# Gate and up products of a gated MLP as seven block products instead of eight, with features and residual kept in DRAM

## The chip, the cores and the metric

The kernel runs on one core of one Trainium2 chip. The metric is device time in microseconds, from the first to the last instruction and what little lies around it; lower is better. One profiled execution supplies the trace.

A core has TensorE (PE, the matrix engine, which writes to the eight banks of PSUM), VectorE (DVE), ScalarE (ACT), GpSimd (POOL) and SyncE (SP), which here issues the DMAs. Each engine runs its own instructions in their order and waits on semaphores. "PEld" are TensorE's weight loads, which lie beside its matmuls.

## The reference

One decoder layer for 1024 tokens of 1024 channels, in float32: a token mixer (two recurrent branches), a layer norm, a gated MLP with a short causal convolution, and a second layer norm. The change concerns the MLP and its surroundings:

```python
def conv_ffn(h, w_gate, w_up, conv_w, conv_b, w_down):
    gate = causal_dwconv(h @ w_gate, conv_w) + conv_b
    return (jax.nn.gelu(gate) * (h @ w_up)) @ w_down
...
x = layer_norm(DEEPNORM_ALPHA * x + (1.0 + gt1) * mix, ln1_g[l], ln1_b[l])
h = x * (1.0 + sc2) + sh2
ff = conv_ffn(h, ffn_w_gate[l], ffn_w_up[l], ffn_conv_w[l], ffn_conv_b[l], ffn_w_down[l])
x = layer_norm(DEEPNORM_ALPHA * x + (1.0 + gt2) * ff, ln2_g[l], ln2_b[l])
```

`D_FF` is 2816, so there are 22 feature tiles of 128; the convolution has three taps.

## The kernel before

Activations lie transposed: 128 channels on the partitions, tokens along the free dimension. There are KT = 8 channel tiles, and the 1024 tokens are cut into two halves of 512, which is what one PSUM bank holds.

**Three matmuls for one.** A float32 product is made of three passes in the type fp32r. `split` (L201, L202) makes from a tile `src` a rounded part `hi` on ACT and the rest `lo = src - hi` on DVE. `mm3` (L268 to L270) then issues hi x hi, hi x lo and lo x hi into one bank. `half_split` does the same for a tile of 512. Weights come by `load_w` (L262): a DMA to a raw buffer, of which there are three, then a split into one of two pairs of buffers, with a priority 1500 instructions ahead.

**Order.** The order of the instructions of each engine is not written out by hand here: a planner orders them when the program is built, by the order of the program (shifted by `high_priority(offset=...)`), by what is ready and by which buffers are free. The chip then keeps that order on each engine. A tile named by `half(...)` is one of 80 buffers of 512 floats in the pool of the third phase, which serves the merge of the two branches, the output projection, both layer norms and the MLP.

**The part before the MLP.** `ys[d][hf]` holds the residual of channel tile d and half hf. For each half, the output projection adds into `ys` (L1070), POOL adds up over d (L996), and `layer_norm_steps` is a generator that issues the norm in 18 steps: the mean by a matmul with a constant matrix (L1007, L1008), the subtraction (L1019), the squares (L1022) and for the second half their sum by 16 matmul instructions with the constant matrix (L1024), the inverse root (L1031, L1032), then for each d the multiplication by it (L1036 on DVE), scale and offset (L1044 on ACT) and `modulate` (L1057 on DVE, then `half_split`), which gives the MLP's input `h2_hi[d][hf]`, `h2_lo[d][hf]`. Callers place these steps between their own work by `steps(ln, n)`; the norm of half 1 lies beside the first feature tiles of half 0.

**The MLP.** The 22 feature tiles are worked in groups of 7, 7 and 8 (`FGROUPS`). `hidden(f, hf, w, carry)` does one tile and one half: the gate product (8 k tiles x 3 matmuls), its copy out of PSUM (L1092), three taps (L1097, L1100, where `carry` brings the last two columns of half 0 to half 1), the GELU on ACT (L1102), the up product, the product of both (L1106) and the split of the result. In the first group all seven tiles of half 0 come before those of half 1; in the second, both halves of a tile follow one another. `down` then multiplies a group's seven or eight feature tiles by a tile of `w_down` and adds into `ys` (L1124), one output tile d after another. The last group's half 0 is followed by its down projection and its norm, which lies beside the last group's half 1; half 1's down projection and norm come last, in two pieces of 256 tokens (`down_and_norm`).

Of the kernel before, what the change touches and what calls it, by code (L numbers as in the profile page):

```python
# [9 lines left out]
F32 = mybir.dt.float32  # L10
# [6 lines left out]
P = 128  # L17
# [14 lines left out]
FGROUPS = (7, 7, 8)  # L32
# [17 lines left out]
N_SIDE0 = 3  # L50
LN_EPS = 1e-5
# [40 lines left out]
def hybrid_layer_kernel(ctx: ExitStack, tc: tile.TileContext, xT, c, w_adaT, cols_in, rows_in,  # L92
# [819 lines left out]
    third = phase("third", 0, 80)  # L912
# [141 lines left out]

    def modulate(d, y, hf, lo):
        t = half("h2")
        V.tensor_scalar(out=t, in0=y, scalar1=mods[:, 16 + d : 17 + d], scalar2=adab[:, 24 + d : 25 + d],  # L1057
                        op0=ALU.mult, op1=ALU.add)
        h2_hi[d][hf], h2_lo[d][hf] = half_split(t)

    ln = iter(())
# [14 lines left out]

    groups = [list(range(sum(FGROUPS[:n]), sum(FGROUPS[: n + 1]))) for n in range(len(FGROUPS))]

    def conv_half():
        return cur["pool"].tile([P, HALF + 4], F32, tag="cv", bufs=4, name=nm("cv"))  # L1080

    def hidden(f, hf, w, carry):

        cv = conv_half()
        if carry is None:
            V.memset(cv[:, 0:4], 0.0)
        else:
            V.tensor_copy(out=cv[:, 2:4], in_=carry)
# [3 lines left out]
        A.activation(cv[:, 4 : 4 + HALF], ps, AF.Copy)  # L1092
        if hf + 1 < NHALF:
            carry = sm([P, 2], tag="carry", bufs=max(FGROUPS) + 1, name="carry")
            V.tensor_copy(out=carry, in_=cv[:, 2 + HALF : 4 + HALF])
        t = half("gate")
        V.tensor_scalar(out=t, in0=cv[:, 2 : 2 + HALF], scalar1=col("ffn_w", 3 * f), scalar2=col("ffn_b", f),  # L1097
                        op0=ALU.mult, op1=ALU.add)
        for i in range(1, 3):
            V.scalar_tensor_tensor(out=t, in0=cv[:, 2 + i : 2 + i + HALF], scalar=col("ffn_w", 3 * f + i), in1=t,  # L1100
                                   op0=ALU.mult, op1=ALU.add)
        A.activation(t, t, AF.Gelu_apprx_tanh)  # L1102
# [4 lines left out]
        return half_split(t), carry  # L1107

    def gate_up(f):
        return [load_w(w_gu[f, s], KT) for s in range(2)]  # L1110
# [4 lines left out]
    def down(fs, acts, d, parts, w=None):  # L1115

        w = w or load_down(fs, d)
# [39 lines left out]
    prev = None  # L1157
    for gi, fs in enumerate(groups):
        acts = [[None] * NHALF for _ in fs]
        ends = gi in (0, len(groups) - 1)  # L1160
        carries = [None] * len(fs)
# [99 lines left out]
```

## Time and the profile before

| | |
|---|---|
| time, median of 3 runs | 2551.51 us (2548.04 to 2556.07) |
| the profiled execution | 2552.6 us, its span 2550.9 us |
| mean granted TensorE clock in it | 0.982 |
| TensorE's matmuls | 11591 |
| output projection ends, MLP begins | about 1790 us into the span |
| last matmul of the down projection | about 2532 us into the span |

The page of the profile gives each engine's busy time and share of the span, then the same in 40 slices, the chain of work that ended last, and the costliest groups of instructions: line, engine, operation, output and inputs, count, then busy time, mean in ns, and the idle time of the engine just before them with what ended it. Busy time of TensorE is modelled (matmuls overlap), so the number of matmuls that start in a stretch says more than its busy share.

### The profile page before, as it was taken

Reading aid. Unit: us, or ns where it says so; the run is one execution under the profiler, and the core shown is the slowest. Engines: PE = TensorE matmul, PEld = TensorE weight load, DVE = VectorE, ACT = ScalarE, POOL = GpSimd, SP = SyncE. Lnnn points to the kernel's source line nnn. Section 1 sums busy time; section 2 is a strip of 40 time slices with the busy share of each in tenths; the row PEclk is TensorE's granted clock in tenths of the full one; section 3 lists DMA queues with packets and bytes.
Section 4 is the critical chain, followed back from the end, with each engine's and each line's share of the span. In section 5 each row is a group of like instructions: output and inputs, shape, how many; then the busy total and the mean of one; then the engine's idle time right before and its main releaser. Section 6 shows DMA issues by size and latency. Waiting matters only on the chain.

```text
span 2550.9 us, 30225 instructions
## 1 busy us (share of the span) xinstructions
PE 2400.5 (94%) x11591; PEld 1974.7 (77%) x11591; DVE 1637.1 (64%) x2624; ACT 1111.4 (44%) x1553; POOL 167.0 (7%) x135
## 2 busy tenths in 40 slices
PE   6989999999989898988888989999999999999997
PEld 4867787788778777777777778878788888888877
DVE  6768999699953377777676446655674244335565
ACT  5555435635633356666665431214543022113354
POOL 3000000000000001011110000004000000000304
PEclk9989999999999999999999999999999999999998
DMA  7346332522363222332234358563232111123333
GB/s 270 128 127 189 114 99 74 166 89 90 90 190 99 66 79 80 98 92 91 75 91 161 118 189 300 194 208 108 78 100 78 54 50 49 51 75 93 98 124 108
DMA packets 160929, 295.47 MB, mean 116 GB/s; under 512 B 63504, under 2 KB 74128, under 8 KB 160272
## 3 DMA queue, kind: packets, MB, share of 16 engines
q1 hardware_dynamic: 160784, 293.54, 36.3%
q8 instruction: 91, 1.49, 0.2%
q14 instruction: 54, 0.44, 0.1%
HBM read 233.65 MB, written 55.64 MB: 113 GB/s over the span
## 4 chain that ended last, share of the span: by engine, by line
PE 73%; DVE 12%; ACT 7%; DMA 4%; issue 3%; SPq 1%; POOL 0%; ACTq 0%; DVEq 0%; POOLq 0%
PE mm L268 21%; PE mm L270 21%; PE mm L269 21%; DVE wl L202 1%; DMA wada<-in_w_adaT 1%; ACT L354 1%; ACT rs L355 1%; ACT rs L354 1%; PE pso L809 1%; PE pd L796 1%; ACT L355 1%; DVE qkv L313 1%; ACT wh L201 1%; DVE tri L534 1%; PE pso L808 1%
## 5 line engine op out<-in xcount | busy, mean ns | idle before, releaser
L268 PE MATMUL mm<-h,wh 128*128 128x512 f32 x1424 | 581.1, 408 | 23.7 <-ACT cv L331 8.1
L268 PE MATMUL mm<-hi,wh 128*128 128x512 f32 (+1 forms) x1536 | 585.9, 384 | 13.0 <-ACT hi L201 8.6
L270 PE MATMUL mm<-hi,wl 128*128 128x512 f32 (+1 forms) x1536 | 583.4, 383 | 3.7 <-DVE wl L202 3.7
L269 PE MATMUL mm<-lo,wh 128*128 128x512 f32 (+1 forms) x1536 | 586.3, 382 | 0.0
L269 PE MATMUL mm<-h,wh 128*128 128x512 f32 x1424 | 562.6, 395 | 1.7 <-DVE h L202 1.7
L270 PE MATMUL mm<-h,wl 128*128 128x512 f32 x1424 | 561.0, 396 | 2.5 <-DVE wl L202 2.3
L201 ACT ACTIVATE wh<-wr 128x1024 fp32r<-128x1024 f32 (+3 forms) x251 | 254.2, 1014 | 568.8 <-PE mm L269 516.4
L202 DVE TENSOR_TENSOR wl<-wr,wh 128x1024 fp32r<-128x1024 f32 (+3 forms) x251 | 297.2, 1185 | 214.0 <-ACT wh L201 210.0
L268 PEld LDWEIGHTS mm<-hi,wh 128*128 128x128 f32 x1536 | 290.2, 189 | 73.3 <-ACT hi L201 11.5
L270 PEld LDWEIGHTS mm<-hi,wl 128*128 128x128 f32 x1536 | 290.4, 189 | 61.4 <-DVE wl L202 5.8
L269 PEld LDWEIGHTS mm<-lo,wh 128*128 128x128 f32 x1536 | 290.4, 189 | 57.2 <-DVE lo L202 1.7
L268 PEld LDWEIGHTS mm<-h,wh 128*128 128x128 f32 x1424 | 272.2, 191 | 78.4 <-ACT cv L331 9.5
L270 PEld LDWEIGHTS mm<-h,wl 128*128 128x128 f32 x1424 | 271.5, 191 | 63.9 <-DVE wl L202 5.5
L269 PEld LDWEIGHTS mm<-h,wh 128*128 128x128 f32 x1424 | 272.4, 191 | 53.0 <-DVE h L202 2.6
L757 POOL TENSOR_TENSOR kg<-kT,eg 128x256 f32<-128x256 f32 x49 | 52.7, 1076 | 1322.2 <-ACT eg L755 1263.4
L1124 DVE SCALAR_TENSOR_TENSOR y<-mm,mods,y 128x512 f32<-128x512 f32 (+1 forms) x56 | 37.6, 674 | 153.7 <-PE mm L270 153.7
L532 DVE TENSOR_TENSOR tmp<-tri 128x62 f32<-128x62 f32 (+30 forms) x124 | 105.9, 854 | 10.0 <-DMA tri<-blk_d 8.6
L313 DVE SCALAR_TENSOR_TENSOR qkv<-cv,cols,qkv 128x1024 f32<-128x1024 f32 x87 | 111.6, 1282 | 0.7
L534 DVE TENSOR_TENSOR tri<-tri,tmp 128x62 f32<-128x62 f32 (+30 forms) x124 | 105.8, 853 | 1.6
L356 DVE TENSOR_TENSOR qkv<-qkv,rs 128x1024 f32<-128x1024 f32 x29 | 35.5, 1225 | 57.9 <-ACT rs L355 57.9
L1100 DVE SCALAR_TENSOR_TENSOR gate<-cv,cols,gate 128x512 f32<-128x512 f32 x88 | 67.1, 763 | 2.7
L1102 ACT ACTIVATE gate<-gate 128x512 f32<-128x512 f32 x44 | 27.7, 630 | 91.7 <-DVE gate L1100 91.7
(272 smaller groups left out, 2911.6 us busy)
## 6 DMA issues: line engine op xcount, KB each, us to landing
wr<-in_w_in SPq DMA_DIRECT2D x81, 512.0 KB, 3.8
wr<-in_w_gu SPq DMA_DIRECT2D x74, 512.0 KB, 3.5
wada<-in_w_adaT SPq DMA_DIRECT2D x64, 256.0 KB, 5.5
wr<-in_w_dn SPq DMA_DIRECT2D x22, 512.0 KB, 3.6
wada<-in_w_adaT SPq DMA_DIRECT2D x16, 512.0 KB, 5.8
decay<-row_d SPq DMA_DIRECT2D x16, 512.0 KB, 5.4
z_d<-z SPq DMA_DIRECT2D x16, 512.0 KB, 4.8
gb<-row_d SPq DMA_DIRECT2D x64, 128.0 KB, 3.2
```

The source lines that it names most:

```text
L201: A.activation(hi, src, AF.Copy)
L202: V.tensor_tensor(out=lo, in0=src, in1=hi, op=ALU.subtract)
L268: T.matmul(ps, w[0][:, kk, :], xh, start=first, stop=False)
L269: T.matmul(ps, w[0][:, kk, :], xl, start=False, stop=False)
L270: T.matmul(ps, w[1][:, kk, :], xh, start=False, stop=last)
L313: V.scalar_tensor_tensor(out=out_t, in0=t[:, o + i : o + i + S], scalar=wcol(i), in1=out_t, op0=ALU.mult, op1=ALU.add)
L354: A.activation(rs, rs, AF.Ln)
L355: A.activation(rs, rs, AF.Exp, scale=-0.5)
L532: V.tensor_tensor(out=tmp, in0=m[:, 0:j, j : j + 1].to_broadcast([P, j, w]), in1=m[:, j : j + 1, j + 1 :].to_broadcast([P, j, w]), op=ALU. ...
L534: V.tensor_tensor(out=m[:, 0:j, j + 1 :], in0=m[:, 0:j, j + 1 :], in1=tmp, op=ALU.add)
L757: (G if i else V).tensor_tensor(out=kg, in0=two(st["k"][:, s]), in1=eg, op=ALU.mult)
L1100: V.scalar_tensor_tensor(out=t, in0=cv[:, 2 + i : 2 + i + HALF], scalar=col("ffn_w", 3 * f + i), in1=t, op0=ALU.mult, op1=ALU.add)
```

## The change

The gate and up weights of a feature tile and the two halves of the input are seen as blocks: the rows are gate and up, the inner dimension is cut into k tiles 0 to 3 and 4 to 7 (KH = 4), the columns are the two halves of tokens. The first three feature tiles (`F_PLAIN`) are done by plain products as before, half 0 and then half 1, with their weights loaded for each half. For the other 19, `seven(f)` forms seven block products of 4 x 3 matmuls, where eight would be the plain scheme. For it, `quarters` loads both weights and forms four sums of weight blocks and splits what the seven products need; `modulate`, when it comes to half 1, forms 16 differences of input tiles (`tq`) with their splits. Three PSUM banks x, y and z are used for each tile, and results that are needed twice are copied or added out of a bank, which then goes on accumulating.

The features are stored to DRAM (`act_d`), as is the residual after the first norm (`y_d`). After all 22 tiles, `residual` loads the residual of a half, and `down_blocks` does the down projection of half 0 and of the first 14 feature tiles of half 1, for six output tiles (`D_BLOCK`) and then two, in chunks of four feature tiles (`F_CHUNK`), each bank accumulating over all feature tiles. The second norm of half 0 lies beside half 1's blocks. The last eight feature tiles of half 1 are done as before, in two pieces of 256 tokens. The first tap of the convolution moves from DVE to ACT. The pool has 74 buffers instead of 80.

```diff
-FGROUPS = (7, 7, 8)
+FT = D_FF // P
+F_PLAIN = 3
+F_TAIL = 8
+F_CHUNK = 4
+D_BLOCK = 6
...
+W_AHEAD = 1500
...
-    third = phase("third", 0, 80)
+    third = phase("third", 0, 74)
...
     def modulate(d, y, hf, lo):
-        t = half("h2")
+        DMA.dma_start(out=y_d[d][hf], in_=y)
+        t = h2[d][hf] = half("h2")
         V.tensor_scalar(out=t, in0=y, scalar1=mods[:, 16 + d : 17 + d], scalar2=adab[:, 24 + d : 25 + d],
                         op0=ALU.mult, op1=ALU.add)
         h2_hi[d][hf], h2_lo[d][hf] = half_split(t)
+        if not hf:
+            return
+        def less(q, k, x, y):
+            r = half("tq")
+            V.tensor_tensor(out=r, in0=x, in1=y, op=ALU.subtract)
+            tq[q][k] = half_split(r)
+            return r
+        k = d % KH
+        if d < KH:
+            t1s.append(less(0, k, t, h2[k][0]))
+        else:
+            less(2, k, t, h2[k][1])
+            less(3, k, h2[d][0], less(1, k, t, t1s[k]))
...
+    def plain(f, hf, cv):
+        w = [load_w(w_gu[f, q], KT) for q in range(2)]
...
+        DMA.dma_start(out=act_d[f][hf], in_=t)
+    def quarters(f):
+        raws = [wpool.tile([P, 8, P], F32, tag="wr", bufs=W_BUFS[0], name=nm("wr")) for _ in range(2)]
+        with tc.high_priority(offset=W_AHEAD):
+            for q, raw in enumerate(raws):
+                DMA.dma_start(out=raw, in_=w_gu[f, q])
...
+            split(gate, hi, lo)
+            res = dict(a11=(hi[:, 0:HALF], lo[:, 0:HALF]), a12=(hi[:, HALF:], lo[:, HALF:]))
+            s1, s2, s3, s4 = (half("ws") for _ in range(4))
+            V.tensor_tensor(out=s1, in0=a21, in1=a22, op=ALU.add)
+            V.tensor_tensor(out=s2, in0=s1, in1=a11, op=ALU.subtract)
+            res["s2"] = half_split(s2)
+            res["s1"] = half_split(s1)
+            V.tensor_tensor(out=s3, in0=a11, in1=a21, op=ALU.subtract)
+            res["s3"] = half_split(s3)
+            V.tensor_tensor(out=s4, in0=a12, in1=s2, op=ALU.subtract)
+            res["s4"] = half_split(s4)
+            res["a22"] = half_split(a22)
+        return res
+    def seven(f):
+        w = quarters(f)
...
+        product(x, w["a11"], b11, True)
+        p1 = kept(x, "p1")
+        product(y, w["a12"], b21, True)
+        plus(cv[:, 4 : 4 + HALF], y, p1)
+        product(x, w["s2"], tq[1], False)
+        u2 = kept(x, "u2")
+        product(z, w["s1"], tq[0], True)
+        p5 = kept(z, "p5")
+        product(x, w["s3"], tq[2], False)
+        up1 = half("up1")
+        plus(up1, x, p5)
+        product(z, w["s4"], b22, False)
+        plus(cv[:, 4 + HALF : 4 + S], z, u2)
+        product(x, w["a22"], tq[3], False)
+        t = cur["pool"].tile([P, S], F32, tag="gate", bufs=2, name=nm("gate"))
+        conv_gelu(f, cv, t, S)
+        V.tensor_tensor(out=t[:, 0:HALF], in0=t[:, 0:HALF], in1=x, op=ALU.mult)
+        V.tensor_tensor(out=t[:, HALF:], in0=t[:, HALF:], in1=up1, op=ALU.mult)
+        for hf in range(NHALF):
+            DMA.dma_start(out=act_d[f][hf], in_=t[:, sl(hf)])
+    cvs = [conv_full() for _ in range(F_PLAIN)]
+    for hf in range(NHALF):
+        for f in range(F_PLAIN):
...
+            plain(f, hf, cvs[f])
+            if not hf:
+                steps(ln, 7)
+        steps(ln, 99)
+    for f in range(F_PLAIN, FT):
+        seven(f)
...
+    def down_blocks(hf, n_f, acts, beside):
+        for d0 in range(0, KT, D_BLOCK):
+            ds = range(d0, min(d0 + D_BLOCK, KT))
+            pss = {d: mm_ps() for d in ds}
+            for f0 in range(0, n_f, F_CHUNK):
+                fs = list(range(f0, min(f0 + F_CHUNK, n_f)))
+                for f in fs:
+                    if f not in acts:
+                        acts[f] = load_act(f, hf)
+                ws = {d: load_part(d, fs) for d in ds}
+                for f in fs:
+                    for d in ds:
+                        mm3(pss[d], ws[d], f - f0, *acts[f], f == 0, f == n_f - 1)
+                steps(beside, 4)
+            for d in ds:
+                with tc.high_priority(offset=EVAC):
+                    V.scalar_tensor_tensor(out=ys[d][hf], in0=pss[d], scalar=mods[:, 24 + d : 25 + d],
+                                           in1=ys[d][hf], op0=ALU.mult, op1=ALU.add)
...
+    residual(0)
+    down_blocks(0, FT, {}, None)
+    total = None
+    for d in range(KT):
+        total = add_up(total, ys[d][0])
+    ln = layer_norm_steps(0, total, "ln2_g", "ln2_b", store)
+    residual(1)
+    down_blocks(1, FT - F_TAIL, {}, ln)
     steps(ln, 99)
+    fs = list(range(FT - F_TAIL, FT))
+    prev = fs, [[None, load_act(f, 1)] for f in fs]
```

`kept` copies a bank to SBUF on ACT and `plus` adds a bank and a tile on DVE, both with a priority 300 instructions ahead; `load_act` and `load_part` load one feature tile or one part of `w_down` (four k tiles for one output tile) and split it; `product` issues three matmuls for each of four k tiles.

More of the change, by code (lines that the diff above doesn't have):

```diff
@@ L1059, in modulate @@
         h2_hi[d][hf], h2_lo[d][hf] = half_split(t)
+        if not hf:
[11 more added lines that the diff above has]
+            less(3, k, h2[d][0], less(1, k, t, t1s[k]))
+    t1s = []
     ln = iter(())
@@ L1074, in hybrid_layer_kernel, with conv_full, conv_gelu @@
         ln = layer_norm_steps(hf, total, "ln1_g", "ln1_b", modulate, hf > 0)
[L1077 to L1088, printed above, removed]
+    def conv_full():
+        return cur["pool"].tile([P, S + 4], F32, tag="cv", bufs=F_PLAIN, name=nm("cv"))
+    def conv_gelu(f, cv, t, n):
+        A.activation(t, cv[:, 2 : 2 + n], AF.Identity, scale=col("ffn_w", 3 * f), bias=col("ffn_b", f))
+        for i in range(1, 3):
+            V.scalar_tensor_tensor(out=t, in0=cv[:, 2 + i : 2 + i + n], scalar=col("ffn_w", 3 * f + i), in1=t,
+                                   op0=ALU.mult, op1=ALU.add)
+        A.activation(t, t, AF.Gelu_apprx_tanh)
+    def plain(f, hf, cv):
+        w = [load_w(w_gu[f, q], KT) for q in range(2)]
+        o = hf * HALF
         ps = mm_ps()
@@ new lines, in product, with kept, plus @@
+    def product(ps, a, bs, first):
+        for k, b in enumerate(bs):
+            c_ = slice(k * P, (k + 1) * P)
+            T.matmul(ps, a[0][:, c_], b[0], start=first and k == 0, stop=False, skip_group_check=not first)
+            T.matmul(ps, a[0][:, c_], b[1], start=False, stop=False, skip_group_check=not first)
+            T.matmul(ps, a[1][:, c_], b[0], start=False, stop=k == KH - 1, skip_group_check=not first)
+    def seven(f):
+        w = quarters(f)
+        b11, b21, b22 = ([(h2_hi[k][hf], h2_lo[k][hf]) for k in ks]
+                         for ks, hf in ((range(KH), 0), (range(KH, KT), 0), (range(KH, KT), 1)))
+        cv = conv_full()
+        V.memset(cv[:, 0:4], 0.0)
+        x, y, z = (mm_ps() for _ in range(3))
+        def kept(ps, name):
+            t = half(name)
+            with tc.high_priority(offset=EVAC):
+                A.activation(t, ps, AF.Copy)
+            return t
+        def plus(out, ps, t):
+            with tc.high_priority(offset=EVAC):
+                V.tensor_tensor(out=out, in0=ps, in1=t, op=ALU.add)
+        product(x, w["a11"], b11, True)
[18 more added lines that the diff above has]
+            DMA.dma_start(out=act_d[f][hf], in_=t[:, sl(hf)])
@@ L1118, in down @@
+    def down(fs, acts, d, parts, w):
         for hf, lo, m in parts:
```

64 lines of the change are left out of this document (29 added, 35 removed).

## The prediction

> **What bounds the kernel now.** I read the page's busy times first, then the busy shares by stretch over the feed-forward part, then the timelines where that part begins and ends.
>
> ```profile
> span 2550.9 us, 30225 instructions
> PE 2400.5 (94%) x11591; PEld 1974.7 (77%) x11591; DVE 1637.1 (64%) x2624; ACT 1111.4 (44%) x1553; POOL 167.0 (7%) x135
> PE 73%; DVE 12%; ACT 7%; DMA 4%; issue 3%; SPq 1%; POOL 0%; ACTq 0%; DVEq 0%; POOLq 0%
> ```
>
> TensorE is busy 94% of the span and holds 73% of the chain that ended last. By stretch (columns: PE, weight loads, DVE, ACT, POOL busy; clock; DMA):
>
> ```profile
> 1836.00:1866.00 30.00, 30.00 (x134) 24.86 (x133) 21.88 (x37) 19.66 (x29) 0.00 (x0) 1.00 0.33 105
> 1900.00:2000.00 100.00, 100.00 (x443) 82.82 (x442) 48.47 (x68) 27.62 (x38) 0.00 (x0) 1.00 0.25 75
> ...
> 2300.00:2400.00 100.00, 100.00 (x443) 82.82 (x442) 46.25 (x63) 29.01 (x36) 16.31 (x7) 1.00 0.32 98
> ```
>
> From 1900 to 2400 TensorE issues 443 matmuls in 100 us, one each 0.2258 us, with no gap and full clock, while DVE has more than half of its time free. Here a matmul less is 0.2258 us less, as long as DVE and ACT keep up.
>
> **What the change removes.** A plain feature tile takes 2 products (gate, up) x 2 halves x 8 k tiles x 3 = 96 matmuls, one done by seven products takes 7 x 4 x 3 = 84. With 19 of 22 tiles done so, 19 x 12 = 228 matmuls go: 228 x 0.2258 = **-51.5 us**. The down projection keeps its 22 x 8 x 2 x 3 = 1056 matmuls (in 512-wide ones), in another order. All matmuls stay 128x512 with one weight load each, so I cost their pace at no change.
>
> **The seven products' own support.** Durations come from the groups of lines between 1900 and 2400 and from the page:
>
> ```profile
> L202 DVE TENSOR_TENSOR wl<-wr,wh 128x1024 fp32r<-128x1024 f32 (+1 forms) x66 | 78.7, 1193 | 76.3 <-ACT wh L201 74.5
> L202 DVE TENSOR_TENSOR lo<-gate,hi 128x512 fp32r<-128x512 f32 x29 | 19.9, 687 | 7.0 <-ACT hi L201 7.0
> L1106 DVE TENSOR_TENSOR gate<-gate,mm 128x512 f32<-128x512 f32 x30 | 20.6, 687 | 48.1 <-PE mm L270 48.1
> L313 DVE SCALAR_TENSOR_TENSOR qkv<-cv,cols,qkv 128x1024 f32<-128x1024 f32 x87 | 111.6, 1282 | 0.7
> L201 ACT ACTIVATE hi<-gate 128x512 fp32r<-128x512 f32 x30 | 19.0, 632 | 27.8 <-DVE gate L1106 27.7
> L201 ACT ACTIVATE wh<-wr 128x1024 fp32r<-128x1024 f32 (+1 forms) x66 | 68.4, 1036 | 253.1 <-PE mm L269 248.9 <-PE mm L270 4.1
> L1092 ACT ACTIVATE cv<-mm 128x512 f32<-128x512 f32 x28 | 16.4, 585 | 28.7 <-PE mm L270 28.7
> ```
>
> Per tile DVE has one 1024-wide split (1.19), four weight sums and five splits (9 x 0.69), three sums out of PSUM and two last products (5 x 0.69) and two taps of 1024 (2 x 1.28): 13.4 us. ACT has the split (1.04), five narrow ones (5 x 0.63), three copies out of PSUM (3 x 0.585) and two passes of 1024 (about 1.04 each): 8.0 us. TensorE takes 84 x 0.2258 = 19.0 us. Both helpers fit (71% and 42%), so this work lies beside the products. If it did not, each us over 19.0 would cost 19 us.
>
> New are four **hand-backs** per tile: bank x serves products 1, 3, 5 and 7, bank z products 4 and 6, and each reuse waits until a copy or sum has read or saved the bank. Between every two stands one product on another bank, 12 x 0.2258 = 2.71 us. A sum behind one tap already running takes 1.28 + 0.69 = 1.97 us and is covered; behind both taps, 2 x 1.28 + 0.69 = 3.25 us, it is 0.54 late. Queued behind such a sum on DVE is the next tile's preparation. Bounds: 0 and one late hand-back per tile, 19 x 0.54 = 10 us (more if the clock falls, below). I take **+4**, nearer to 0, since the next tile's first two products need no hand-back and can run into a wait.
>
> **Where it begins.** Now seven tiles of half 0 (76 us) cover the layer norm of half 1; after, three do. Two timelines, DVE and ACT, and the chain with PE's averaging matmuls:
>
> ```profile
> 1829.26 3.44 PE pre L1024 x8
> 1822.13 0.58 ACT L1092 ACTIVATE cv<-mm 128x512 f32<-128x512 f32 x1
> ...
> 1834.40 1.23 DVE L202 TENSOR_TENSOR wl<-wr,wh 128x1024 fp32r<-128x1024 f32 x1 [8.42 <-ACT wh L201]
> 1836.35 4.91 DVE L1036 TENSOR_TENSOR y<-y,rs 128x512 f32<-128x512 f32 x8 [0.72 <-ACT rs L1032]
> ...
> 1846.50 0.54 DVE L1057 TENSOR_SCALAR h<-y,mods,adab 128x512 f32<-128x512 f32 x1
> ...
> 1864.52 0.69 DVE L202 TENSOR_TENSOR lo<-h,hi 128x512 fp32r<-128x512 f32 x1 [0.62 <-ACT hi L201]
> 1865.13 0.54 DVE L1097 TENSOR_SCALAR gate<-cv,cols 128x512 f32<-128x512 f32 x1
> ```
>
> The third tile's gate product is copied at 1822.13; its 24 up matmuls (5.4) and 16 averaging ones (3.44 per 8, so 6.9) end at 1834.5, and after the change TensorE then wants half 1 of the input. But DVE starts to normalise half 1 only at 1836.35. It then has 8 multiplications (4.91, 0.61 each), 8 modulations (0.5 each, 4.0) and 8 splits (4.9), and the change puts into the same loop 16 differences, each with a split. The last row shows that DVE keeps the order of the program: the third tile's convolution, ready since 1822.7, waited until every modulation was done, though DVE stood idle 8.42 us before 1834.4. So I take the differences where the code has them, ahead of the next k tile: 13 of them before the last k tile's split, 13 x 2 x 0.61 = 15.9. With two weight splits (2.3) the last of half 1 is ready at 1836.35 + 4.9 + 4.0 + 4.9 + 15.9 + 2.3 = 1868.4. In the meantime TensorE can only take the first tile's gate and up, six matmuls per k tile, so it ends these at about 1869.8; undisturbed it would have at 1834.5 + 48 x 0.2258 = 1845.3. That is **+24.5 us**. Bounds: +8.6 if all splits came before the differences (24.5 - 15.9), +36 if DVE is held up by ACT as it is now, busy 21.88 of the 30 us from 1836 to 1866 (32.05 x 30 / 21.88 = 44, so 11.9 more). The loop also queues 16 stores of the residual on SP, each behind its y, and weight loads behind them; the loads of the first two tiles have landed by then, so that is nothing, or one landing if not.
>
> Then both weights are released at once, as they are at the start of the first tile:
>
> ```profile
> 1801.99 1.07 ACT wh L201
> ...
> 1803.08 1.24 DVE wl L202
> ...
> 1804.36 0.51 PE mm L270
> ```
>
> The second tile's weights are split only then, 1804.36 - 1801.99 = 2.4 us in which TensorE gets two matmuls: **+2**. Bounds 0 and 2.4.
>
> **The second layer norm.** TensorE now stops once beside it, and its clock falls:
>
> ```profile
> 2440.62 0.50 PE L270 MATMUL mm<-hi,wl 128*128 128x512 f32 x1 [1.98 <-DVE wl L202]
> 2442.10 0.43 PE mm L269
> ...
> 2444.66 0.43 PE mm L269
> ...
> 2445.92 0.24 PE mm L270
> ```
>
> After a gap of 2.37 us between starts, some eight matmuls come 0.43 us apart: 2.1 + 8 x 0.2 = 3.7 us lost. After the change this norm lies beside 14 feature tiles of the down projection (336 matmuls, 76 us), which ask DVE for only ten 0.69 us splits per 72 matmuls (16.3 us). I take **-3.5**; bounds -3.7 and 0.
>
> A rule that speaks against the change: the Trainium skill, TensorE: Matmul & The Clock Gate, section "A second HAM failure mode: psum-queue depth-cycling", says that small idle times between groups of matmuls, as banks are cycled, can make the clock fall to half and rise again and again. The trace so far does not bear it out: six banks are cycled between 1900 and 2400 at clock 1.00. By the rule the hand-backs would cost more than their gaps; that is the slower rival below.
>
> **Through DRAM.** Features go out and come back 256 KB at a time, the residual too, and each half loads the down weights itself. A chunk of the first block brings 4 features and 6 weight parts, 10 x 262 KB = 2.62 MB per 72 matmuls (16.3 us), 161 GB/s. The highest stretch of now moves 283:
>
> ```profile
> 1498.00:1600.00 102.00, 101.25 (x442) 82.98 (x441) 66.44 (x134) 29.04 (x45) 0.00 (x0) 0.99 0.81 283
> rec<-rec_d SPq DMA_DIRECT2D x20, 256.0 KB, 4.9
> ```
>
> So the rate is covered; the first chunk is not wholly. Its features and parts get buffers as the last tile's products free theirs, then need a landing (4.9) and a split (0.63 + 0.69), 6.2 us of the 19.0. Queued with them on SP are the last tile's stores. I take **+3** for this entry and **+2** for the later chunk ends, where 44 feature and 12 weight buffers leave few free; bounds 0 and 6.2 each.
>
> **Six buffers fewer** (80 to 74) in the pool that serves the merge, too. It ends now with TensorE short of work:
>
> ```profile
> 1694.00:1706.00 12.00, 8.54 (x33) 6.06 (x33) 8.87 (x23) 3.16 (x4) 0.00 (x0) 0.94 0.51 175
> ```
>
> 33 matmuls where 12 / 0.2258 = 53 fit, 4.5 us lost to waits for loads. Fewer buffers may lengthen or reorder this: bounds -4.5 and +9 (as much twice more), taken **+2**.
>
> **Sum:** -51.5 + 4 + 24.5 + 2 - 3.5 + 3 + 2 + 2 = -17.5. The profiled execution took 2552.6 (span 2550.9 and 1.7 around it), the median of the runs is 2551.5: 2551.5 - 17.5 = **2534 us**.
>
> **The rivals.**
> *Differences hidden.* If the order leaves the differences until after the splits of half 1, the entry costs 8.6 and not 24.5: 2534 - 15.9 = 2518. For it: the next 22 us of plain products leave DVE room. Against: the row at 1865.13.
> *Longer entry.* If the loop also waits for ACT at each step, +36 for 24.5: 2546, no change. For it: ACT has three passes more for a late k tile, too. Against: DVE has other ready work in each wait.
> *Hand-backs slow the clock* (the slower side). One late hand-back per tile, 0.54, followed by the fall of the clock seen at 2442 (8 x 0.2 = 1.6): 2.14 x 19 = 41 in place of 4, so 2571. For it: DVE at 71% in strict order, with two taps of 1.28 back to back. Against: free products to fill in. It decides from (17.5 + 4) / 19 = 1.1 us per tile.
> *Loads bind the down projection.* At the span's mean of 116 GB/s a chunk of 2.62 MB takes 22.6 us and not 16.3; nine such chunks, +57: 2591. Against: 283 GB/s above.
> That the products are not fewer can't be: their number is fixed by the code.
>
> **How the numbers follow.** Chances: forecast (2520 to 2543) 0.48, differences hidden 0.22, longer entry 0.14, slow hand-backs 0.12, loads 0.04. About 0.3% (7.7 us) is what a measurement can tell from no change. Faster: 0.48 + 0.22 and a little of the third, 0.72; slower: the last two, 0.16; the same, 0.12. The range leaves out the last two rivals' ends and the best end of the second: 2508 to 2560.
>
> **What would show it.** Right: 84 matmuls per 19.0 us with no gap in the middle of the seven products; a stretch of some 25 to 30 us with six matmuls per k tile and DVE full, some 45 us into the feed-forward part; no gap over 3 us where the down projection begins. Wrong: matmuls 0.43 us apart inside the seven products; half 1's splits ahead of the differences; TensorE waiting for feature loads.

## The result, and the profile after

| | before | after |
|---|---|---|
| time, median | 2550.79 us (4 runs, 2548.04 to 2556.07) | 2622.13 us (4 runs, 2617.01 to 2624.26) |
| profiled execution: time, span | 2552.6, 2550.9 us | 2621.5, 2619.8 us |
| matmuls recorded | 11591 | 11363 |

The changed kernel is **slower by 2.7%**: the ratio is 1.0274, its 95% interval 1.0252 to 1.0297. 2534 us were forecast, with 2560 as the upper end.

In rows of the changed kernel the splits are L206 (ACT) and L207 (DVE), `mm3` is L273 to L275, the seven products are L1163 to L1165, the copies out of their banks L1179, the sums L1184, a tile's Identity and Gelu L1113 and L1117, the norm's averages L1012 and L1013. First the top of the page, engines and chain:

```profile
span 2619.8 us, 30516 instructions
PE 2380.5 (91%) x11363; PEld 1937.9 (74%) x11363; DVE 1712.0 (65%) x2747; ACT 1188.1 (45%) x1701; POOL 165.4 (6%) x135
PE 62%; DVE 16%; ACT 9%; DMA 7%; issue 4%; SPq 1%; POOL 0%; DVEq 0%; ACTq 0%; POOLq 0%
```

The 228 matmuls are gone (11591 - 11363), and the span still grew. DVE and ACT hold a larger part of the chain that ended last (they had 12% and 7%): TensorE now waits for its helpers. The busy shares by stretch (columns: stretch, length, busy time of PE, weight loads, DVE, ACT, POOL, then the clock, DMA share and GB/s) say where:

```profile
1836.00:1887.00 51.00, 24.47 (x54) 14.27 (x52) 35.85 (x57) 25.00 (x37) 0.00 (x0) 0.62 0.18 62
...
1906.00:2268.00 362.00, 350.19 (x1525) 284.57 (x1523) 221.28 (x322) 142.38 (x201) 0.00 (x0) 1.00 0.26 78
...
2298.00:2400.00 102.00, 90.18 (x386) 73.49 (x386) 42.33 (x64) 38.00 (x63) 0.00 (x0) 0.95 0.48 155
2400.00:2620.00 220.00, 175.50 (x890) 147.05 (x890) 99.76 (x159) 77.74 (x127) 55.27 (x44) 0.91 0.37 118
```

In the kernel before, stretches of this part had PE at 100%. Now it is short of work where half 1 comes in, a little in the seven products, and in the down projection. No helper is full in any of these rows: in the last one DVE is busy 45% and ACT 35%, the DMAs 37%. What is missing is not their capacity.

From the starts of matmuls the loss can be laid out by stage, each against 0.2258 us per matmul. The span grew by 68.9 us though 51.5 us of matmuls went, so 120.4 us of waits came in:

| stage | took | its matmuls alone | lost | forecast |
|---|---|---|---|---|
| merge, 74 buffers | | | about 3 | 2 |
| plain tiles of half 1, 1836.4 to 1911.0 | 74.6 | 144 x 0.2258 = 32.5 | 42.1 | 24.5 + 2 |
| nineteen tiles of seven products, 1911.0 to 2297.6 | 386.6 | 1595 x 0.2258 = 360.1 | 26.5 | 4 |
| entry into the down projection | 10.65 | 0.2 | 10.4 | 3 |
| down projection with the second norm, the rest of 120.4 | | | about 38 | 2 - 3.5 |

**Half 1 comes in.** TensorE's timeline, then DVE's (start, length, engine, line, operation, and in brackets how long the engine stood idle before and on what):

```profile
1882.79 1.22 PE L273 MATMUL mm<-hi,wh 128*128 128x512 f32 x2 [5.06 <-ACT hi L206]
```

```profile
1873.48 0.54 DVE L1072 TENSOR_SCALAR h<-y,mods,adab 128x512 f32<-128x512 f32 x1
1874.77 0.69 DVE L207 TENSOR_TENSOR lo<-h,hi 128x512 fp32r<-128x512 f32 x1 [0.75 <-ACT hi L206]
1875.38 0.69 DVE L1080 TENSOR_TENSOR tq<-h,h 128x512 f32<-128x512 f32 x1
1876.82 0.69 DVE L207 TENSOR_TENSOR lo<-tq,hi 128x512 fp32r<-128x512 f32 x1 [0.76 <-ACT hi L206]
...
1882.77 0.69 DVE L207 TENSOR_TENSOR lo<-h,hi 128x512 fp32r<-128x512 f32 x1 [0.76 <-ACT hi L206]
```

The rows show a strict alternation: subtract on DVE, round on ACT, take the rest on DVE, with DVE idle 0.69 to 0.76 us in each round while it waits for ACT. A difference costs 2.05 us (1876.82 - 1874.77), not the 1.22 of its two DVE instructions. Each of the last k tiles of half 1, with three differences between it and the next, then takes 8 us (1882.77 - 1874.77), for six matmuls.

**The seven products.** TensorE's timeline over one tile, the rows of L1165 except the last. `wl` stands in products 1 and 2, `lo` in the others:

```profile
2018.50 0.39 PE L1165 MATMUL mm<-hi,wl 128*128 128x512 f32 x1
2019.18 0.39 PE L1165 MATMUL mm<-hi,lo 128*128 128x512 f32 x1
...
2021.22 0.39 PE L1165 MATMUL mm<-hi,lo 128*128 128x512 f32 x1
2021.44 0.39 PE L1165 MATMUL mm<-hi,wl 128*128 128x512 f32 x1
...
2023.48 0.39 PE L1165 MATMUL mm<-hi,wl 128*128 128x512 f32 x1
...
2026.20 0.39 PE L1165 MATMUL mm<-hi,lo 128*128 128x512 f32 x1
2027.28 0.50 PE L1163 MATMUL mm<-hi,hi 128*128 128x512 f32 x1 [0.69 <-ACT u L1179]
```

Between products 1 and 2 stands another product, four k tiles long. It can only be the fourth, on bank z: the planner moved it ahead. So products 3 and 5, both on bank x, follow each other, and the copy `u2` between them is laid bare: 1.08 us from start to start, once every 20.02 us, in 17 tiles with next to no variation. The clock stays 1.00 (second row of the stretches).

The last of the 19 tiles has five gaps, one of them a late hand-back of 2.54 us between starts, and behind that one the matmuls come 0.43 us apart:

```profile
2284.25 0.50 PE L1163 MATMUL mm<-hi,hi 128*128 128x512 f32 x1 [2.16 <-ACT p L1179]
...
2285.31 0.63 PE L1163 MATMUL mm<-hi,hi 128*128 128x512 f32 x1
2285.74 0.63 PE L1164 MATMUL mm<-lo,hi 128*128 128x512 f32 x1
```

The granted clock is 0.50 there from 2284.7 to 2288.1. The gaps of 10.65 us at 2308 and of 3.48 to 11.79 us in the down projection are followed by such slow matmuls, too.

**The down projection begins.** TensorE, SP's queue and ACT:

```profile
2297.61 0.39 PE L1165 MATMUL mm<-hi,lo 128*128 128x512 f32 x1
2308.26 0.80 PE L273 MATMUL mm<-hi,wdh 128*128 128x512 f32 x1 [10.26 <-ACT wdh L206]
```

```profile
2301.81 0.92 SPq L1205 DMA_DIRECT2D act_d<-gate  x2
2302.82 0.91 SPq L1222 DMA_DIRECT2D act<-act_d  x2
2303.83 2.75 SPq L1229 DMA_DIRECT2D wdr<-in_w_dn  x6
```

```profile
2300.01 1.06 ACT L1117 ACTIVATE gate<-gate 128x1024 f32<-128x1024 f32 x1 [2.67 <-DVE gate L1115]
2300.97 1.13 ACT L206 ACTIVATE hi<-act 128x512 fp32r<-128x512 f32 x2
```

The last tile's stores (L1205) wait for its last product, and the first weight parts (L1229) stand behind them in SP's queue. On ACT the splits of the first weight parts stand behind the last tile's Gelu.

**The second norm.** TensorE, ACT and DVE in the chunk that ends with the norm's second average:

```profile
2502.23 0.40 PE L1013 MATMUL pre<-lo,mean_r 128*128 128x512 f32 x1
2514.01 0.79 PE L273 MATMUL mm<-hi,wdh 128*128 128x512 f32 x1 [11.39 <-ACT wdh L206]
```

```profile
2502.70 1.28 ACT L1036 ACT_TABLE_LOAD   x1 [17.06 <-PE pre L1013]
...
2510.74 2.91 ACT L1049 ACTIVATE y<-y,cols 128x512 f32<-128x512 f32 x4
2513.56 0.40 ACT L206 ACTIVATE wdh<-wdr 128x256 fp32r<-128x256 f32 x1
```

```profile
2485.67 0.69 DVE L207 TENSOR_TENSOR lo<-sum,hi 128x512 fp32r<-128x512 f32 x1 [3.52 <-ACT hi L206]
2506.66 4.90 DVE L1041 TENSOR_TENSOR y<-y,rs 128x512 f32<-128x512 f32 x8 [20.29 <-ACT rs L1037]
```

The operand of the average was ready at 2486.4. In TensorE's order the average stands behind the whole chunk, so it ran at 2502.2. Until then ACT was idle 17 us while TensorE worked; then ACT had 11 us to do, nearly all of it the norm's, with the next chunk's weight splits behind it, and TensorE was idle 11.8 us. The two engines took turns. The first average, at 2458.8, has the same picture at half the size (5.68 + 2.09 us).

**The end of a block of output tiles.** DVE at the end of half 0's six output tiles:

```profile
2393.33 0.75 DVE L1253 SCALAR_TENSOR_TENSOR y<-mm,mods,y 128x512 f32<-128x512 f32 x1 [13.26 <-PE mm L275]
2394.00 0.42 DVE L207 TENSOR_TENSOR wdl<-wdr,wdh 128x256 fp32r<-128x256 f32 x1
```

The addition of a finished bank to the residual (L1253) waits for TensorE's last product on that bank, and the next weight split stands behind it on DVE. TensorE waits for that split: five gaps of 1.1 to 1.4 us at 2393 to 2405. The gaps of 1.62 and 3.48 us at 2437 to 2440 have the same picture (L1253 waits 17.28 us there). This is read from the order in the trace; no run moved these additions.

From 2308 to 2533 TensorE lost 45 us against its pace: 33 in 14 gaps, and 11 in some 50 matmuls behind these gaps, which start 0.3 us or more apart.

### The profile page after: what moved, and what is told of

Same layout as the page of the kernel before. It is cut to its first block, busy times and chain, and to the rows that moved or that the text cites. A ratio compares the mean times of both kernels' runs of the same rounds, so it can differ in the third digit from the quotient of the medians.

```text
span 2619.8 us, 30516 instructions
## 1 busy us (share of the span) xinstructions
PE 2380.5 (91%) x11363; PEld 1937.9 (74%) x11363; DVE 1712.0 (65%) x2747; ACT 1188.1 (45%) x1701; POOL 165.4 (6%) x135
## 4 chain that ended last, share of the span: by engine, by line
PE 62%; DVE 16%; ACT 9%; DMA 7%; issue 4%; SPq 1%; POOL 0%; DVEq 0%; ACTq 0%; POOLq 0%
PE mm L275 14%; PE mm L273 14%; PE mm L274 14%; PE mm L1163 4%; PE mm L1165 4%; PE mm L1164 4%; DVE wl L207 2%; DVE lo L207 1%; DMA wada<-in_w_adaT 1%; ACT L359 1%; ACT wh L206 1%; DVE qkv L318 1%; ACT rs L360 1%; ACT rs L359 1%; DMA invT_d<-tmpT 1%
## 5 line engine op out<-in xcount | busy, mean ns | idle before, releaser
L273 PE MATMUL mm<-h,wh 128*128 128x512 f32 x1424 | 580.7, 408 | 24.9 <-ACT sg L566 8.4
L275 PE MATMUL mm<-h,wl 128*128 128x512 f32 x1424 | 561.1, 396 | 2.3 <-DVE wl L207 2.1
L206 ACT ACTIVATE wh<-wr 128x1024 fp32r<-128x1024 f32 (+2 forms) x184 | 184.7, 1006 | 380.9 <-PE mm L274 268.2
L207 DVE TENSOR_TENSOR wl<-wr,wh 128x1024 fp32r<-128x1024 f32 (+2 forms) x184 | 218.2, 1187 | 198.5 <-ACT wh L206 196.2
L273 PEld LDWEIGHTS mm<-h,wh 128*128 128x128 f32 x1424 | 272.3, 191 | 79.3 <-ACT sg L566 9.6
L275 PEld LDWEIGHTS mm<-h,wl 128*128 128x128 f32 x1424 | 271.3, 191 | 63.9 <-DVE wl L207 5.3
L273 PE MATMUL mm<-hi,wh 128*128 128x512 f32 (+1 forms) x640 | 239.8, 385 | 40.3 <-ACT hi L206 36.1
L274 PE MATMUL mm<-lo,wh 128*128 128x512 f32 (+1 forms) x640 | 241.4, 379 | 1.9 <-DVE lo L207 1.9
L275 PE MATMUL mm<-hi,wl 128*128 128x512 f32 (+1 forms) x640 | 238.8, 379 | 3.1 <-DVE wl L207 3.1
L273 PEld LDWEIGHTS mm<-hi,wh 128*128 128x128 f32 x640 | 122.2, 194 | 71.8 <-ACT hi L206 44.4
L1163 PE MATMUL mm<-hi,hi 128*128 128x512 f32 x380 | 150.9, 397 | 16.4 <-ACT u L1179 12.5
L1165 PE MATMUL mm<-hi,lo 128*128 128x512 f32 x380 | 148.7, 391 | 0.7 <-DVE lo L207 0.7
L274 PEld LDWEIGHTS mm<-lo,wh 128*128 128x128 f32 x640 | 123.8, 193 | 26.7 <-DVE lo L207 5.8
L275 PEld LDWEIGHTS mm<-hi,wl 128*128 128x128 f32 x640 | 123.8, 194 | 26.2 <-DVE wl L207 5.1
L273 PE MATMUL mm<-hi,wdh 128*128 128x512 f32 x288 | 116.8, 405 | 28.9 <-ACT wdh L206 28.9
L275 PE MATMUL mm<-hi,wdl 128*128 128x512 f32 x288 | 117.0, 406 | 10.4 <-DVE wdl L207 10.4
```

Of the source, the lines that this page charges most:

```text
L206: A.activation(hi, src, AF.Copy)
L207: V.tensor_tensor(out=lo, in0=src, in1=hi, op=ALU.subtract)
L273: T.matmul(ps, w[0][:, kk, :], xh, start=first, stop=False)
L274: T.matmul(ps, w[0][:, kk, :], xl, start=False, stop=False)
L275: T.matmul(ps, w[1][:, kk, :], xh, start=False, stop=last)
L1163: T.matmul(ps, a[0][:, c_], b[0], start=first and k == 0, stop=False, skip_group_check=not first)
```

## The experiments

The kernel before was run beside them on each chip: 2548.3 us in the first two batches, 2551.95 and 2552.42 as medians later, single runs between 2547.85 and 2557.09. Up to the three repairs, differences are to the changed kernel's profiled run, 2621.5 us. Most experiments ran once, and one kernel's runs lie up to 11 us apart (the seven together, below), so a single time tells nothing under about 10 us; where less matters, the gap in the trace is read.

### One wait at a time

**Late differences.** `modulate` only normalises and splits; the differences go behind the plain tiles of half 1.

```diff
-        if d < KH:
-            t1s.append(less(0, k, t, h2[k][0]))
-        else: ...
+    def differences(k): ...
...
             if not hf:
                 steps(ln, 7)
+            else:
+                for k in ((0, 1), (2,), (3,))[f]:
+                    differences(k)
```

> The changed kernel with the 16 input differences and their splits issued beside the plain products of half 1 instead of inside the loop that makes half 1. Theory A (the differences in the loop, each waiting for ACT, hold half 1 back): the first tile's gate and up of half 1, which now end at 1887 us, end some 25 us earlier (8 k tiles at 1.85 us, as for half 0), and the time falls by 22 to 30 us to about 2595. Rival (the loop is bound by the norm's own steps, or the differences are merely late elsewhere): the end moves by under 8 us, or the same 25 us come back as a wait of the first seven-product tiles.

2600.4 us, 21 less, just under Theory A's 22 to 30. After the first wait of 6.6 us, which stayed, half 1's first tile came through nearly undisturbed: it ended at 1855 and not at 1887. But 15.6 us returned where the seven products begin, as the rival's second half has it. TensorE and DVE there:

```profile
1898.26 0.79 PE L1158 MATMUL mm<-hi,hi 128*128 128x512 f32 x1 [15.26 <-ACT hi L206]
```

```profile
1895.01 0.69 DVE L207 TENSOR_TENSOR lo<-tq,hi 128x512 fp32r<-128x512 f32 x1 [0.74 <-ACT hi L206]
1895.62 0.69 DVE L1143 TENSOR_TENSOR ws<-wr 128x512 f32<-128x512 f32 x1
```

The place of the differences was the cause of the wait at half 1, all but its first 6.6 us. The first tile's weight sums (L1143) now stand behind the last of them.

**Stores on POOL's queue.**

```diff
-        DMA.dma_start(out=y_d[d][hf], in_=y)
+        G.dma_start(out=y_d[d][hf], in_=y)
```

and in the same way for `act_d` and the first half of `out`.

> The changed kernel with the stores of residual, features and half 0's output issued from POOL's queue instead of SP's. Theory Q (a store that waits for its data holds the loads behind it on SP's queue): the gap of 10.65 us where the down projection begins and the one of 11.78 us beside the second norm shrink to under 4 us each, the time falls by 12 to 22 us to about 2605. Rival B (the loads wait for free buffers, which the products release late): both gaps stay within 3 us of what they are, and the time within 8 us.

2616.7 us, a difference within the noise, so the trace decides: the gap at the entry fell from 10.65 to 6.11 us (with a new one of 1.14 behind it), that beside the norm stayed (11.79). Theory Q is half right. The stores held the loads for some 4 us of the entry; SP's queue has no part in the norm's wait.

**TensorE's products as written.**

```diff
-    for f in range(F_PLAIN, FT):
-        seven(f)
+    with tc.manual_schedule(engines={mybir.EngineType.PE}):
+        for f in range(F_PLAIN, FT):
+            seven(f)
```

> The changed kernel with TensorE's matmuls of the 19 seven-product tiles kept in the order of the program, so that product 4 stands between products 3 and 5. Theory H (products 3 and 5 follow each other on bank x, and the copy between them is laid bare): a tile takes 19.0 to 19.3 us instead of 20.0 and the time falls by 13 to 19 us to about 2606. Rival (the third product waits for its weights, which is why the planner moved it): 19.6 us or more per tile, with the wait at product 3 on ACT or DVE splits of the weight sums.

2599.8 us, 22 less, a little more than Theory H's 13 to 19. The gaps of 1.08 us are gone (five of 0.7 to 1.0 are left, in 19 tiles), the last tile's five went with them, some 6 us, and the stretch is 20 us shorter:

```profile
1911.00:2278.00 367.00, 363.77 (x1590) 296.97 (x1589) 229.50 (x333) 146.57 (x207) 0.00 (x0) 1.00 0.30 91
```

With four hand-backs a tile still there, but each behind another product, all 19 tiles lose 8 us (367.0 - 1590 x 0.2258), near the forecast's 4 and within its bounds. The forecast's picture holds for the order in the code, not for the order that the planner made.

**Four output tiles at a time** (`D_BLOCK = 4` for 6).

> The changed kernel with four output tiles at a time in the down projection's blocks instead of six and two. Rival B (free buffers are short at the ends of chunks: 44 for features and 12 for weights): 4 buffers more are free, the gaps of 1.1 to 1.6 us around 2393 to 2405 and 2435 to 2440 go, and the down projection is 6 to 15 us shorter. Theory Q (the queue alone): these gaps stay, and the time is within 5 us; the gaps at the beginning and beside the norm stay under both.

2613.9 us, inside what a single run can tell. In the trace the five gaps of 1.1 us at 2393 to 2405 became three, as the additions of four banks would have it; the pair at 2437 stayed, and so did those beside the norm (5.68 and 10.49). This speaks against a shortage of buffers.

**The norm apart**, behind the blocks of half 1:

```diff
                         mm3(pss[d], ws[d], f - f0, *acts[f], f == 0, f == n_f - 1)
-                steps(beside, 4)
```

> The changed kernel with nothing beside the down projection of half 1: the second norm of half 0 is emitted after that projection's blocks instead of four steps per chunk. Theory N (the averaging matmul at a chunk's end makes ACT and DVE, in their fixed order, wait for TensorE with the next chunk's splits behind them): the gaps of 5.7+2.1 us at 2459-2466 and of 11.8+2.5 us at 2502-2517 go, about 20 us in all, and some 17 instructions of the norm land at the end beside the last eight features' products, so 2602 to 2612. Rival R (the norm's work must lie somewhere, and the tail has as little room): the gaps reappear in the last 100 us, 2618 to 2625. Rival S (the chunk ends wait for loads): the gaps stay, 2620.

2627.1 us, nearest to Rival R (2618 to 2625). The norm's gaps in the blocks went, and others came behind the blocks, where the norm now stands, the first and longest of them:

```profile
2538.68 0.80 PE L1012 MATMUL pre<-hi,mean_r 128*128 128x512 f32 x1 [12.36 <-ACT hi L206]
```

This alone does not tell the place of the averages from a lack of room for the norm.

### Do they add up?

**Three repairs:** late differences, POOL's queue, products as written.

> Late differences, stores on POOL's queue and TensorE's products as written, all three together. If the three waits are separate: 2621 - 21 - 22 - 5 = 2573, with a range of 2568 to 2578. If the wait of 15.6 us at the first seven-product tile came from the planner's order of the products as well, 2558 to 2565. If a repair only moves a wait to the next, above 2585.

2590.7 us, not 2573: a repair handed its wait on. The wait at the first seven-product tile had grown from 15.6 to 20.8 us. ACT's timeline there:

```profile
1901.60 0.63 ACT L206 ACTIVATE hi<-tq 128x512 fp32r<-128x512 f32 x1 [1.41 <-DVE tq L1078]
...
1909.55 0.61 ACT L206 ACTIVATE hi<-wr 128x512 fp32r<-128x512 f32 x1
1910.07 0.58 ACT L1174 ACTIVATE p<-mm 128x512 f32<-128x512 f32 x1
```

The copy of product 1 (L1174, 0.58 us) waits behind the splits of the differences and of the whole tile's weights, though its bank was ready long before: TensorE had stopped at 1889.9.

**The first tile's weights early:** the differences' four groups behind the first two plain tiles (three and one), and the first such tile's `quarters` right behind them, ahead of the third plain tile. The expectation tells the place a little otherwise: the weights stood ahead of the last plain tile, not of the last group.

> As the three repairs together, with the sums and splits of the first seven-product tile's weights emitted ahead of the last difference group, after the second plain tile of half 1. If the wait at the first seven-product tile is the weight sums behind the differences on DVE, 12 to 15 us less than the three repairs (2558 to 2562). If it is the differences themselves that come late, no change; if half 1's plain tiles lose their cover, up to 10 us more.

2594.0 us, and the gap was still 17.8 us. The edit didn't bring about what the expectation is about: on DVE the first weight sum still started at 1905.46, right behind the last difference's split at 1904.85. So it leaves open whether sums ahead of the differences would have helped. The time that all these splits take was the next suspect.

**Part of the first chunk early:** one feature tile and two output tiles' weights ahead of the last seven-product tile.

> As the three repairs together, with one feature tile and two output tiles' weights of the down projection's first chunk emitted ahead of the last seven-product tile. If the wait at the entry (6.1 us with the stores on POOL's queue) is the order of ACT, whose splits of these parts sit behind the last tile's Identity and Gelu, 4 to 6 us less than the three repairs. If it is the load, or the room of the 74 buffers, no change within 2 us.

2604.9 us, worse. The entry's gap fell from 6.06 (the three repairs) to 3.98, but a new one of 8.0 us opened in the last tile, again before a copy on ACT behind splits of that tile's weights.

**The norm spread**, one step after each feature tile:

```diff
                     for d in ds:
                         mm3(pss[d], ws[d], f - f0, *acts[f], f == 0, f == n_f - 1)
-                steps(beside, 4)
+                    steps(beside, 1)
```

> The three repairs, and the second norm's steps one after each feature tile of the down projection of half 1 instead of four at a chunk's end, so that its two averages stand inside a chunk. Theory N2 (it is the place of the averages in TensorE's order: at a chunk's end the next chunk's splits sit behind the norm on ACT and DVE, and TensorE has nothing left to do): the gaps of 5.7+2.1 and 11.8 us go, 2590.7 - 18 = 2573, range 2570 to 2578. Rival (ACT and DVE have no room for the norm there at all, as with the norm apart): the gaps move, 2588 to 2595.

2588.7 us, no change: the gaps were 5.01 + 2.08 and 11.78. The edit hadn't brought about what the expectation needs. The planner had put the second average at the chunk's end again:

```profile
2471.74 0.40 PE L1013 MATMUL pre<-lo,mean_r 128*128 128x512 f32 x1
2483.52 0.79 PE L273 MATMUL mm<-hi,wdh 128*128 128x512 f32 x1 [11.39 <-ACT wdh L206]
```

**Four plain tiles**, with one group of differences beside each (`F_PLAIN = 4`, 71 buffers).

> The three repairs, with four plain feature tiles instead of three, one group of differences beside each in half 1, and 71 buffers instead of 74 for the fourth convolution tile. Theory C (the wait of 20.8 us at the first seven-product tile is ACT's copy behind the splits of the late differences, which end at 1903 us; a fourth plain tile gives them time): 12 matmuls more by 0.2258 = +2.7 us, and the 20.8 us go down to 0 to 4, so 2590.7 - 15 to 18 = 2573 to 2576. Rival (buffers: 71 are too few for the differences beside four plain tiles): the time comes back as waits in the plain tiles, above 2585.

2573.8 us, as expected in time, but partly by luck: the gap there went from 20.8 to 12.0, not to 4. The rest of the 17 us came from elsewhere, above all from the wait of 6.6 us where half 1 begins, which is gone in this trace and which the expectation doesn't name.

**The last tile's end late:** its convolution, Gelu, last products and stores behind the first chunk's loads.

> The three repairs, with the last feature tile's convolution, Gelu, products and stores, and the reloads of the residual, emitted behind the loads and splits of the down projection's first chunk. If the wait of 6.1 us there is ACT's order (Identity and Gelu of the last tile ahead of the first splits), 4 to 6 us less than the three repairs, 2585 to 2587. If it is the loads themselves, no change.

2593.6 us. The gap at the entry was 4.98 us for 6.06, and a second one 0.89 for 1.14. That doesn't clear ACT's order, for on ACT the order had changed only in part:

```profile
2278.86 1.06 ACT L1112 ACTIVATE gate<-gate 128x1024 f32<-128x1024 f32 x1 [2.11 <-DVE gate L1110]
...
2280.34 3.21 ACT L206 ACTIVATE wdh<-wdr 128x512 fp32r<-128x512 f32 x6
```

Three of the four features' splits now stood ahead of the last tile's Gelu, but the splits of all six weight parts still stood behind it. The first part was asked for at 2267.4 and a landing took at most 7.1 us, so it lay ready from 2274.5 on. ACT stood idle for 2.11 us, waiting for the last tile's taps on DVE, with the splits behind. So the wait that was left goes with ACT's order and not with the loads, as far as the trace tells; no run took the Gelu out of the way.

**Seven together:** late differences, POOL's queue, products as written, four plain tiles, the norm spread, the last tile's end late, four output tiles at a time.

> All of it: the three repairs, four plain tiles, the norm spread, the last tile's end late, and four output tiles at a time. If the waits are separate: 2590.7 - 16 - 18 - 5 - 7.5 = 2544, range 2540 to 2556, level with the kernel before; with all waits gone and 51.5 - 2.7 us of matmuls less it could reach no lower than about 2503. If each repair only hands the wait on, above 2565.

2572.2 us (4 runs, 2566.5 to 2577.6), ratio to before 1.0082, interval 1.0062 to 1.0101. Still slower than the kernel before and far from 2544: 12.0 us were left at the first seven-product tile, 5.7 + 2.1 and 10.5 us beside the norm, and 5.0 at the entry.

### The two waits that were left

**The averages in place:** the spread, with TensorE's order of the blocks of half 1 as written.

```diff
-    down_blocks(1, FT - F_TAIL, {}, ln)
+    with tc.manual_schedule(engines={mybir.EngineType.PE}):
+        down_blocks(1, FT - F_TAIL, {}, ln)
```

> The norm spread, with TensorE's instructions of the down projection of half 1 kept in the written order, so that the two averages really stand after the first and second feature tile of a chunk: with the spread alone the second average still started at 2471.5 us, 16 us after its operand, at the end of a chunk. Theory N2 (the place of the average on TensorE holds ACT and DVE, and the next splits behind them): the gap of 11.8 us goes and of the 5.0+2.1 us most, 2588.7 - 14 to 18 = 2571 to 2575. Rival (the norm's own 11 us on ACT, table loads, Ln, Exp and eight scalings, have no room in any place): the gaps stay within 3 us, 2585 to 2591.

2567.1 us, 21.5 less than with the spread alone, a little more than expected. TensorE's timeline:

```profile
2455.39 0.40 PE L1013 MATMUL pre<-lo,mean_r 128*128 128x512 f32 x1
...
2463.59 0.39 PE L275 MATMUL mm<-hi,wdl 128*128 128x512 f32 x1
2465.86 0.50 PE L273 MATMUL mm<-hi,wdh 128*128 128x512 f32 x1 [1.88 <-ACT wdh L206]
```

ACT does the same norm, with the same table loads; 8 us of matmuls are now left behind the average, and of 11.8 us 2.3 remain. Those at the first average are gone. The edit keeps all of TensorE's instructions of these blocks in order, and three more gaps of 1.1 to 1.5 us behind them went with it. But ACT's and DVE's work is the same, so the large gaps come from the place of the averages on TensorE and not from a lack of room.

**Subtractions first:** on the three repairs, the four subtractions of a group, and the four sums of a tile's weights, ahead of their splits.

```diff
-        t1 = less(0, k, h2[k][1], h2[k][0])
-        ...
+        t1 = less(h2[k][1], h2[k][0])
+        t2 = less(h2[k + KH][1], t1)
+        t3 = less(h2[k + KH][1], h2[k][1])
+        t4 = less(h2[k + KH][0], t2)
+        for q, r in enumerate((t1, t2, t3, t4)):
+            tq[q][k] = half_split(r)
```

> The three repairs, with the four subtractions of a difference group, and the four sums of a tile's weights, emitted ahead of their splits. If the chain between DVE and ACT (0.7 us idle at every change of engine, 16 times and 4 times) is what makes the first seven-product tile late: the last difference's split lies 8 to 10 us earlier than 1902.9 us and the gap of 20.8 us shrinks to 9 to 13, 2590.7 - 8 to 12 = 2579 to 2583. If it is DVE's sheer work, 2588 to 2592.

2579.6 us, 11 less, and the gap 9.09 us for 20.83. DVE there, same instructions as before, back to back:

```profile
1896.24 1.29 DVE L207 TENSOR_TENSOR lo<-tq,hi 128x512 fp32r<-128x512 f32 x2
1897.45 0.69 DVE L1145 TENSOR_TENSOR ws<-wr 128x512 f32<-128x512 f32 x1
...
1899.98 2.49 DVE L207 TENSOR_TENSOR lo<-ws,hi 128x512 fp32r<-128x512 f32 x4
```

No idle time stands before any row. So the chain of changes between DVE and ACT made up more than half of the wait. The 9 us that are left lie beside a DVE that works without a pause from 1885 to 1903: that part goes with its work.

**Those seven with both:**

> All repairs together with the averages in place and the subtractions first. From 2572 (2566.5 in the profiled run): the 12.0 us at the first seven-product tile down to 0 to 4, the 5.7+2.1 and 10.5 us beside the second norm down to 0 to 4: 2572 - 16 to 24 = 2548 to 2556, level with the kernel before. Rival (every wait removed lays the next one bare): above 2562.

**2541.7 us** (5 runs, 2540.1 to 2543.9); to the kernel before, 2552.4 us (8 runs), the ratio is **0.9956, interval 0.9940 to 0.9972**. So it is 0.4% faster than the kernel before, little but clear of 1 by this interval. The top of its page:

```profile
span 2540.0 us, 30678 instructions
PE 2364.0 (93%) x11375; PEld 1934.6 (76%) x11375; DVE 1708.4 (67%) x2740; ACT 1187.6 (47%) x1700; POOL 195.3 (8%) x203
```

DVE and ACT do what they did in the slow version, 1708 and 1188 us for 1712 and 1188. What differs is the order, the queue of the stores, the size of the blocks and a fourth plain tile (twelve matmuls more), and 80 us (2622.1 - 2541.7) went with it. Of the 48.8 us that its 216 fewer matmuls are worth, 10.7 arrive; the longest gaps left in the MLP are 4.1 us at the first seven-product tile, 5.0 at the entry into the down projection, 1.7 + 3.5 where half 1 begins there, and 5.0 at 2416. At the entry the first weight split (2247.25) stands behind the last tile's Gelu (2245.76) once more.

## Why the prediction was wrong

- **The matmuls removed (-51.5).** Right: 228 fewer in the trace, and their pace is 0.2258 us where the clock is full. Behind long stops it is 0.43 us. The forecast counted that for the old norm and for its slower rival only; here it cost another 11 us in the down projection.
- **Hand-backs (+4; 26.5 lost).** The step that failed is "Between every two stands one product on another bank": it read the code's order as TensorE's. The planner's order put products 3 and 5 side by side. About 18 of the 26.5 us are that (17 x (20.02 - 84 x 0.2258)), shown by the run with the products as written; some 6 lie in five gaps of the last tile, which went in that run too, and 2 in the slow matmuls behind the longest of them.
- **The clock at the hand-backs (the slower rival).** Refuted but for one tile: 17 stops of 1.08 us, one per 20.02 us, at clock 1.00 from 1906 to 2268. The Trainium skill, TensorE: Matmul & The Clock Gate, section "A second HAM failure mode: psum-queue depth-cycling", lets such small stops pull the clock down; stops this short and this far apart did not. The one hand-back with a stop of 2.54 us, in the last tile, did have slow matmuls behind it. The kernel came out on the slower side for other reasons.
- **Half 1 comes in (+24.5 and +2; 42.1 lost).** The mechanism was right, the size not. Forecast was the last split at 1868.4; it started at 1882.8, and these 14.4 us are nearly all of the 15.6 that were missed. The mis-sized term is "13 x 2 x 0.61 = 15.9": a difference took 2.05 us and not 1.22, since DVE idles 0.7 us while ACT rounds, and the split of h itself has the same idle time. This is what the rival *longer entry* said; its 11.9 us more would have put the last split at 1880.3. The argument against it, "DVE has other ready work in each wait", was wrong, as the order on DVE left almost nothing else to run.
- **The second norm (-3.5; about 20 lost, 5.68 + 2.09 + 11.78 + 2.54 less four paces of 0.23 = 21.2).** This step failed by its sign. It weighed DVE's load per chunk (16.3 us of TensorE, ten splits), which was indeed small. It didn't ask where in each engine's order the averages and the next chunk's splits stand. The run with the averages in place shows that this was the cause of nearly all of it: 2.3 us of gaps are left there.
- **Entry into the down projection (+3; 10.4 lost).** "Queued with them on SP are the last tile's stores" named the queue but gave it no price: some 4 us, by the run with the stores elsewhere. The forecast left out ACT's order at this place, where the first weight splits stand behind the last tile's Gelu. The 5 us that are still there in the best version go with that by its trace; it isn't shown by a run.
- **Later chunk ends (+2).** Too small: five gaps of 1.1 to 1.4 us at 2393 to 2405 and one of 1.6 + 3.5 at 2437, all for a DVE split: 10.9 us, or 9.3 without their pace of 0.23 each. The forecast looked for these waits in short buffers. By the trace they come from DVE's order, the split behind a bank's addition to the residual; four output tiles at a time left three of the five small ones. No run tested the order itself.
- **74 buffers (+2).** The merge's end lost about 3 us more (gaps of 4.76 and 2.00 us at 1701 to 1708 for 3.10, 0.95 and 0.90 before, and slow matmuls behind them). Every trace with 74 buffers has such gaps, but no run set the changed kernel back to 80, so it isn't shown that the buffers are the cause.
- **Loads as the bound (2591).** Refuted: the DMAs are busy 37% to 48% in the down projection, and no stage follows their rate.

One mechanism is behind most of the large misses: a short instruction on a helper engine that stands behind another one which itself waits. At the hand-backs it was TensorE's own order. The forecast compared busy times with the time available and took what fits as free.

## What to carry to other kernels

When an edit takes work from the engine that binds and gives some to engines that are half idle, add up not only the work but the places: for each helper instruction that TensorE will wait for, read what stands ahead of it in that engine's order, and what that in turn waits for. A reduction that TensorE does for a norm belongs in the middle of a stretch of matmuls, as soon as its operand is ready; at the end of a stretch its followers on other engines run alone. Where a value goes from one engine to another and back, issue several first steps before the first second step; and look at the order that the planner made, not at the one in the code.

## What the runs showed of the hardware

- A split chain DVE, ACT, DVE cost 0.69 to 0.76 us of idle DVE per round for 128x512 tiles, more than the 0.63 us of the ACT instruction in between; four rounds issued together cost none (the run with the subtractions first, 1896 to 1902).
- TensorE ran at clock 1.00 through one stop of 1.08 us every 20 us, but at 0.62 in the stretch 1836 to 1887, where it had 54 matmuls in 51 us. A single stop of 2.54 us, 2.16 of them idle, was followed by 3.4 us at clock 0.50.
